# Where the products of the next block's input stand on VectorE, and one step less for two projection units, in a chunked-attention stage

## The chip, the cores and the metric

The kernel runs on one core of a Trainium2 chip. The metric is the time of one execution on the device in microseconds (us); lower is better. Of several runs of one kernel the median is taken. One execution is also recorded by the hardware profiler, and all durations of single instructions come from such a record. The engines are TensorE (PE in the profile; its weight loads are PEld), VectorE (DVE), ScalarE (ACT), GpSimd (POOL) and SyncE (SP), which here only issues DMAs.

## The reference

One layer over 2048 frames of width 1024. A normalised input feeds one projection; its first 512 columns go through a state-space layer, the other 1536 are queries, keys and values of chunked attention. Both outputs are normalised, go through one output projection, and a gated feed-forward network follows. What matters here is the input of the attention and the attention:

```python
h = rmsnorm(x, norm_mix_g[l])
proj = h @ w_in[l]
...
scores = jnp.einsum('bnqhd,bnkhd->bhnqk', qc, kb) / math.sqrt(HEAD_DIM)
scores = scores + bias[None, :, None, :, :]
scores = jnp.where(valid[None, None, :, None, :], scores, -1e30)
probs = jax.nn.softmax(scores, axis=-1)
out = jnp.einsum('bhnqk,bnkhd->bnqhd', probs, vb)
```

There are 8 heads of 64 columns; a frame attends to its own chunk of 64 frames and the 8 chunks before it. All of it is float32.

## The kernel before, in words

**Phases.** The kernel computes the state-space input first, then attention together with the state-space scan, then the output projection, the feed-forward network and the final norm. Every float32 matmul operand is split into a part `hi` (cast to a 32-bit format that PE takes in one pass) and the rest `lo`; `mm3` (L145 to L148) makes three matmuls of each product: hi by hi, hi by lo, lo by hi. All PE instructions of this stage are kept in program order; for the other engines a scheduler decides the order of their queues when the kernel is built, by when it thinks that each operand is ready. An instruction can so be queued long before the place at which the program names it.

**Attention in steps.** `att_phase` (L687) works through 128 steps: 4 blocks of 512 frames, 4 pairs of heads in each, 2 heads of a pair, 4 groups of 128 queries. Block *b* has the steps 32*b* to 32*b*+31; "step 23 of block 1" is step 55. Step *s* does, in this order (`ORDER`, L52):

- the scores of step *s* (L848): two to four matmuls into the PSUM tile `sc`, of which there is one; then on DVE one instruction (L874) that adds the bias and takes the minimum `mn` of each row; then on ACT the exponential (L877). Scores are negated, so that the minimum is what is subtracted.
- after the fourth query group of a head, the product with the values (L895), three steps late, and the scaling of a finished pair (L919), four steps late.
- the transposes of step *s*-2 (L880): up to five on PE into the one tile `pt`, then a cast `pth` on ACT (L892) and a difference `ptl` on DVE (L893).
- pieces of the units that are due (L984 to L986).

**Units.** A `Unit` (L665) is a generator with a number of pieces, a first step and a step by which it is over; `advance` (L672) runs as many pieces in each step as the share of its steps that has gone by. They fill PE between scores and transposes:

- `qk_unit(sb, pr)` (L754): queries and keys of one pair of heads, 2 x 8 pieces of three matmuls. When the key half is over, ACT casts the keys into `k2` (L799) and DVE forms the difference (L800); the scores of that pair read `k2`. In block 0 a scaling (L784) goes before it.
- `v_unit(sb, fh)` (L807): values of four heads, 16 pieces of six matmuls.
- `hT_unit(sb, q0, q1)` (L724): the normalised input of block `sb`, eight tiles `q` of 128 rows. It loads a tile (into `xt`, or two at a time into `raw`), and multiplies it on DVE by the gain and the row scale, in place (L749: the product); ACT casts it to `hi` (L750) and DVE forms `lo` (L751). Its first three tiles are due in steps 20 to 22 of the block before, the other five in steps 24 and 25. The next block's first `qk_unit` begins in step 24 and reads tiles 0 to 2 there, 3 to 5 in step 25, 6 and 7 in step 26.
- `ssm_front` (L561) and `ssm_back` (L636): eight parts of the scan. Each has a few matmuls (`pj<-U,Bst`, `pj<-U,Tm`), copies on ACT, and about 37 us of small operations on POOL (L598 to L610), of which the last eight (L609, L610 on 434 columns) are the long ones.

The tuple `CUT` (L50) says at which steps of a block the units begin and end: pair 0 from -8 to -2, values' first half to 2, pair 1 to 7, pair 2 to 13, values' second half to 19, pair 3 (the last) to 24. `CUTL` is the same for the last block but ends pair 3 at 23. Pair 3's scores begin at step 24.

## Time and profile before

| | us |
|---|---|
| median of 3 runs | 2253.35 |
| lowest and highest | 2246.03, 2255.34 |
| the profiled execution | 2247.43 |
| its span (first to last instruction) | 2245.7 |
| attention stage, 128 steps, from about | 136 to 702 |

A row of the timeline is: start in us from the span's start, duration in us, engine, line, operation, what it writes and reads, shape, count, and in brackets how long the engine was idle before it and what ended that. A row of a group has a count, and minimum, median and maximum duration in ns. A row of the windows has the length of the window, then the busy time and number of instructions of PE, PEld, DVE, ACT and POOL, then the clock of PE that was granted (1.00 is full), the share of the DMA engines and GB/s. Matmuls overlap, so that the distance from one start to the next says more than the duration of one: 128x512 matmuls last 0.39 us and start 0.23 us apart.

### The profile page before, as it was taken

The numbers are of one execution on the slowest core, as the hardware profiler recorded it, in microseconds if no ns is written. First come the engines' busy times: TensorE is split into PE (matmuls) and PEld (weight loads), VectorE is DVE, ScalarE is ACT, GpSimd is POOL, SyncE is SP. The second block draws the span as 40 slices with busy tenths as digits, with TensorE's granted clock in tenths as the row PEclk, the third lists the DMA queues.
The fourth block names the chain that finished last, engine by engine and source line by source line (L and its number), as shares of the span: only waits on it lengthen the run. The fifth ranks groups of instructions, "written<-read, shape, count | busy, mean of one in ns | idle before, by whom it ended". The sixth has DMA issues, their size and how long they took to land.

```text
span 2245.7 us, 30154 instructions
## 1 busy us (share of the span) xinstructions
PE 2155.6 (96%) x10632; PEld 1817.4 (81%) x10632; DVE 1543.3 (69%) x2706; ACT 1004.6 (45%) x1667; POOL 352.4 (16%) x827
## 2 busy tenths in 40 slices
PE   8998899999997999999999999999999999999997
PEld 6777788899986788788888887888888788888886
DVE  7756666555557766777766678767666477689776
ACT  5455555556557642443333335333333343353322
POOL 2246576656500000000000000000000100000000
PEclk9999999999998999999999999999999999999999
DMA  8878876666652435845655557646333395465652
GB/s 281 251 244 275 280 220 204 202 192 199 190 166 99 155 113 181 288 136 155 198 168 194 191 182 268 210 144 213 117 100 112 122 383 192 160 228 177 220 175 76
DMA packets 194744, 430.16 MB, mean 192 GB/s; under 512 B 19872, under 2 KB 38352, under 8 KB 187488
## 3 DMA queue, kind: packets, MB, share of 16 engines
q1 hardware_dynamic: 186944, 403.32, 54.4%
q0 software_dynamic: 7648, 24.92, 3.6%
q8 instruction: 83, 1.36, 0.2%
q14 instruction: 69, 0.57, 0.1%
HBM read 288.95 MB, written 131.10 MB: 187 GB/s over the span
## 4 chain that ended last, share of the span: by engine, by line
PE 81%; DVE 7%; DMA 4%; ACT 3%; issue 2%; SPq 0%; DVEq 0%; ACTq 0%
PE X L76 20%; PE ps L76 19%; PE Y L76 10%; PE pf L76 10%; PE big L76 7%; PE W L76 5%; PE pj L76 4%; PE pt L79 2%; PE sc L76 2%; DMA lo<-hc 1%; DMA xt<-in_xt 1%; DVE ptl L893 1%; DMA x<-xt 0%; DVE s L874 0%; DVE lo L153 0%
## 5 line engine op out<-in xcount | busy, mean ns | idle before, releaser
L76 PE MATMUL X<-hi,c 128*128 128x512 f32 x1408 | 449.8, 390 | 6.7 <-DVE c L153 3.9
L76 PE MATMUL ps<-hd,hd 128*128 128x512 f32 (+1 forms) x1968 | 428.1, 379 | 3.1 <-DVE hd L153 2.0
L76 PEld LDWEIGHTS ps<-hd,hd 128*128 128x128 f32 x1968 | 356.4, 188 | 73.3 <-DVE hd L153 2.7
L76 PEld LDWEIGHTS X<-hi,c 128*128 128x128 f32 x1408 | 264.5, 188 | 63.2 <-DVE c L153 4.7
L76 PE MATMUL X<-lo,c 128*128 128x512 f32 x704 | 274.4, 390 | 0.0
L153 ACT CAST hd<-hd 128x1536 fp32r<-128x1536 f32 (+1 forms) x106 | 147.5, 1394 | 229.9 <-DMA hd<-hq 175.5
L76 PE MATMUL Y<-hi,c 128*128 128x512 f32 x704 | 224.8, 390 | 3.1 <-DVE u L1421 2.5
L153 DVE TENSOR_TENSOR hd<-hd 128x1536 fp32r<-128x1536 f32 (+1 forms) x106 | 174.0, 1643 | 38.0 <-ACT hd L153 37.7
L153 DVE TENSOR_TENSOR c<-S,c 128x512 fp32r<-128x512 f32 x176 | 120.8, 687 | 100.1 <-ACT c L153 99.8
L1525 POOL DMA_DIRECT2D hd<-hq x7 | 5.3, 755 | 1161.5 <-PE X L76 1148.8
L1417 ACT COPY u<-X 128x512 f32<-128x512 f32 x132 | 77.3, 586 | 197.7 <-PE X L76 197.7
L153 ACT CAST c<-S 128x512 fp32r<-128x512 f32 x176 | 109.4, 621 | 120.5 <-PE Y L76 61.6
L76 PE MATMUL big<-m,woh 128*128 128x512 f32 x512 | 160.1, 394 | 0.0
L76 PEld LDWEIGHTS Y<-hi,c 128*128 128x128 f32 x704 | 132.4, 188 | 31.9 <-DVE u L1421 3.3
L1559 DVE TENSOR_TENSOR acc<-acc,ps 128x512 f32<-128x512 f32 x196 | 129.6, 680 | 37.3 <-PE ps L76 37.1
L76 PEld LDWEIGHTS X<-lo,c 128*128 128x128 f32 x704 | 132.4, 188 | 27.4
L76 PE MATMUL pf<-hi,w 128*128 128x512 f32 x416 | 149.3, 411 | 0.0
L153 ACT CAST c<-raw 128x512 fp32r<-128x512 f32 x132 | 82.2, 623 | 147.7 <-PE Y L76 70.6
L76 PE MATMUL Y<-lo,c 128*128 128x512 f32 x352 | 137.2, 390 | 0.0
L893 DVE TENSOR_TENSOR ptl<-pt,pth 128x640 fp32r<-128x640 f32 (+3 forms) x152 | 98.2, 646 | 55.2 <-ACT pth L892 53.8
L877 ACT ACTIVATE s<-s,mn 128x640 f32<-128x640 f32 (+4 forms) x128 | 98.0, 765 | 61.1 <-DVE mn L874 57.7
L892 ACT CAST pth<-pt 128x640 fp32r<-128x640 f32 (+3 forms) x152 | 83.6, 550 | 84.2 <-PE pt L79 79.5
(448 smaller groups left out, 4267.9 us busy)
## 6 DMA issues: line engine op xcount, KB each, us to landing
w<-wss SPq DMA_DIRECT2D x36, 1024.0 KB, 6.1
hq<-g SPq DMA_DIRECT2D x140, 256.0 KB, 2.1
hd<-hq SPq DMA_DIRECT2D x35, 768.0 KB, 4.4
hd<-wc SPq DMA_DIRECT2D x35, 768.0 KB, 5.9
raw<-in_w_gate SPq DMA_DIRECT2D x44, 512.0 KB, 3.7
raw<-in_w_up SPq DMA_DIRECT2D x44, 512.0 KB, 4.1
wc<-px SPq DMA_DIRECT2D x66, 256.0 KB, 3.4
wss<-w SPq DMA_DIRECT2D x12, 1024.0 KB, 6.0
```

The costliest lines, as they stand in the source:

```text
L76: return self.tc.keep_in_program_order(self.tc.nc.tensor.matmul(*a, **b))
L79: return self.tc.keep_in_program_order(self.tc.nc.tensor.transpose(*a, **b))
L153: return nc.scalar.copy(hi, raw), nc.vector.tensor_tensor(lo, raw, f32(hi), op=ALU.subtract)
L877: nc.scalar.activation(s[:, :nk], s[:, :nk], AF.Exp, bias=mn[:], scale=-1.0, accum_out=sums[sb, pr][:, hh, qp : qp + 1])
L892: nc.scalar.copy(pth[:, a:b, qp, :], pt[:, a:b, :])
L893: nc.vector.tensor_tensor(ptl[:, a:b, qp, :], pt[:, a:b, :], f32(pth[:, a:b, qp, :]), op=ALU.subtract)
L1417: nc.scalar.copy(u[:], ps[:])
L1525: (nc.gpsimd if aside else nc.sync).dma_start(f32(lo), src.rearrange("g p c -> p g c"))
L1559: V.tensor_tensor(a, a, ps[:], op=ALU.add)
```

## The change

Three things change, all in the attention stage. L749, the product of the next block's input, is put behind the latest L874 that the program has named at that point, in DVE's queue: the minimum of the step in which `hT_unit` is advanced. The values' second half ends at step 18 in place of 19, and pair 3 runs from step 18 to 23 in place of 19 to 24. And the last block takes the same cuts as the others, so that its pair 3 has the steps 18 to 23 in place of 19 to 23. No computation is added or left out.

```diff
-CUT = -8, -2, 2, 7, 13, 19, 24
-CUTL = -8, -2, 2, 7, 13, 19, 23
+CUT = -8, -2, 2, 7, 13, 18, 23
...
-                nc.vector.scalar_tensor_tensor(xt, xt, k.gm[:, q : q + 1], S["rsn"][:, ts], op0=ALU.mult, op1=ALU.mult)
+                with tc.issue_after(k.least):
+                    nc.vector.scalar_tensor_tensor(xt, xt, k.gm[:, q : q + 1], S["rsn"][:, ts], op0=ALU.mult, op1=ALU.mult)
...
-            nc.vector.tensor_tensor_reduce(
+            ins = nc.vector.tensor_tensor_reduce(
                 s[:, :nk].rearrange("p (a b) -> p a b", a=nch), ps[:, :nch, :half],
                 hd.nb[:, nk - 1 :: -1].rearrange("p (a b) -> p a b", a=nch), 1.0, 3e38, ALU.add, ALU.min, mn[:])
+            k.least = ins.ins
...
-            C = CUT if sb < NSB - 1 else CUTL
+            C = CUT
```

`issue_after` asks the scheduler to place the instructions of its block later in the queue of the same engine than the one it names. It adds an order, and no semaphore.

## Prediction
> **What bounds the kernel now.** I read the page first: one engine fills the span.

> ```profile
> span 2245.7 us, 30154 instructions
> PE 2155.6 (96%) x10632; PEld 1817.4 (81%) x10632; DVE 1543.3 (69%) x2706; ACT 1004.6 (45%) x1667; POOL 352.4 (16%) x827
> ```

> TensorE (PE) is busy 96% of the span, so a scheduling edit can only win back moments in which PE stands still or runs slowly. The change acts in the attention stage alone. I cut that stage into its four blocks; the cuts are the starts of the instructions number 32, 64 and 96 of L874, which runs once a step. The busy times stand in the order PE, PEld, DVE, ACT, POOL.

> ```profile
> 267.00:421.00 154.00, 144.80 (x881) 130.35 (x880) 100.27 (x165) 86.50 (x176) 101.41 (x233) 0.98 0.70 216
> 421.00:558.00 137.00, 136.69 (x867) 124.81 (x866) 78.21 (x141) 78.86 (x158) 87.70 (x235) 1.00 0.67 202
> ```

> Block 1 (first row) and block 2 do the same attention work; block 2 leaves PE 0.3 us idle, block 1 leaves 9.2 us (154.00 less 144.80) and has a lower granted clock (0.98). So block 1 is where something is to be had. Next, the view of L749, the product that the change moves.

> ```profile
> L749 DVE SCALAR_TENSOR_TENSOR xt<-xt,g_mix,rsn x12: 741/751/1549, 214.9 to 390.2; 128x512 f32<-128x512 f32 x12
> L749 DVE SCALAR_TENSOR_TENSOR raw<-raw,g_mix,rsn x12: 740/745/2132, 237.4 to 392.7; 128x512 f32<-128x512 f32 x12
> ```

> The last products start at 392.7 us, in block 1, though what they make is block 3's input and block 3 starts at 558 us. The products run wherever their input lands and DVE's queue has them, not where the step order puts them. The timeline shows what that does in step 2 of block 1:

> ```profile
> 279.30 2.13 DVE L749 SCALAR_TENSOR_TENSOR raw<-raw,g_mix,rsn 128x512 f32<-128x512 f32 x1
> 281.42 1.07 POOL L609 TENSOR_TENSOR fx<-X,a 128x434 f32<-128x434 f32 x1
> 282.17 0.87 DVE L749 SCALAR_TENSOR_TENSOR raw<-raw,g_mix,rsn 128x512 f32<-128x512 f32 x1
> 282.96 0.81 DVE L893 TENSOR_TENSOR ptl<-pt,pth 128x640 fp32r<-128x640 f32 x1
> 283.83 1.26 PE L79 MATMUL pt<-ident,s 128*128 128x128 f32 x5 [3.11 <-DVE ptl L893]
> ```

> PE waits 3.11 us for `ptl`, which stands in DVE's queue behind two products (2.13 and 0.87 us) that nobody needs for another 90 us. Then the last pair's projection. In blocks 0 and 1 it ends in step 23, and step 24's scores read its keys at once; the rows are block 0, then block 1:

> ```profile
> 227.86 0.58 SPq L654 DMA_DIRECT2D y<-U  x1
> 232.01 0.69 DVE L784 TENSOR_TENSOR yt<-pf,rsn 128x512 f32<-128x512 f32 x1 [0.28 <-PE pf L76]
> 232.95 0.34 SPq L566 DMA_DIRECT2D U<-u  x1
> 233.38 1.40 DVE L800 TENSOR_TENSOR k<-yt,k 64x512 fp32r<-64x512 f32 x2 [0.68 <-ACT k L799]
> 234.17 0.30 PE L76 MATMUL sc<-k,q2h 128*128 128x128 f32 x1 [2.20 <-issue]
> 239.59 3.64 PE L76 MATMUL pj<-U,Bst 128*128 128x256 f32 x8 [2.61 <-DMA Bst<-bsts]
> ...
> 375.00 1.08 DVE L749 SCALAR_TENSOR_TENSOR xt<-xt,g_mix,rsn 128x512 f32<-128x512 f32 x1
> 376.00 2.98 DVE L751 TENSOR_TENSOR lo<-raw,hi 128x512 fp32r<-128x512 f32 x2
> 379.02 0.68 DVE L800 TENSOR_TENSOR k<-pf,k 64x512 fp32r<-64x512 f32 x1
> 379.76 0.63 PE L76 MATMUL sc<-k,q2h 128*128 128x320 f32 x1 [4.09 <-DVE k L800]
> ```

> In block 0 PE waits 2.20 us while the keys are evacuated (L784, L799, L800); in block 1 it waits 4.09 us, because L800 stands behind one product and two `lo` differences. The two long waits of block 1 cost more than themselves. The column before the last two is the granted clock:

> ```profile
> 284.00:287.30 3.30, 3.30 (x11) 2.81 (x11) 3.23 (x6) 1.51 (x3) 1.23 (x2) 0.50 0.51 118
> 379.60:382.90 3.30, 3.14 (x11) 2.81 (x12) 2.74 (x6) 1.72 (x3) 3.20 (x4) 0.50 0.53 196
> ```

> After each of them some 3.3 us run at half clock, which is 1.7 us of lost work.

> **The change part by part.** No instruction is added or removed but the order; the queue behind each L749 and the steps of two units move.

> *Early products go (L749 behind this step's L874).* Block 2's eight products leave steps 1 to 4 of block 1. The 3.11 us wait and its half clock go: **-4.8 us**. Block 2 at the same steps has next to no PE idle, so nothing else is late there. Ends: 0 (if `ptl` is late for another reason) and -4.8; I take -4.8, since the two products in front of `ptl` last 3.0 us of the 3.11.

> *Last pair a step sooner (18 to 23).* The key evacuation of 1.4 us and what is before it then lies beside step 23. Block 1: 4.09 and 1.7 go, **-5.8 us**. Block 0: the 2.20 goes, but 2.8 us later PE stands before `U,Bst` anyway, for a transfer: `U<-u` is issued only when the store `y<-U` has landed (issued 227.86, next 232.95). PE comes to it sooner and waits longer, unless the store moves too. It was issued behind the queries' copies of the last pair on SP's queue, which now come a step sooner, but the matmuls that fill `U` (step 20) have three projection groups more ahead of them. Ends 0 and -2.2; I take **-1.0**, the middle, as no row is nearer to one end.

> *Values' second half in five steps in place of six.* PE does the same matmuls; denser steps 13 to 17 have PE as their limit: 0. It also starts the scan of steps 16 to 25 a little later on POOL (79% of the half lies before its matmuls in step 16, against 68%), which counts below. For block 3 the pair takes five steps in place of four with the same end: 0. Of the DMAs, the weight loads of the moved units and the copies of keys and queries go one step earlier on SP's queue; the landing that PE waits for in these steps is the one of block 0 above.

> *What is late next: step 23 without a projection.* Scores and transposes alone then. Block 3 has such steps today; the three rows below it are block 2's scan matmuls:

> ```profile
> 661.59 0.41 PE L76 MATMUL sc<-k,q2h 128*128 128x320 f32 x1 [1.12 <-DVE mn L874]
> ...
> 520.37 1.89 PE L76 MATMUL pj<-rsn,Bst 128*128 128x256 f32 x8
> 525.63 0.59 PE L76 MATMUL pj<-U,Tm 128*128 128x256 f32 x2
> 528.90 0.50 PE L76 MATMUL sc<-k,q2h 128*128 128x320 f32 x1
> ```

> The next scores wait 1.12 us for the minimum that reads the one `sc` tile. Block 2 has 1.89 us of scan matmuls in step 23 as cover (and 3.3 us, from 525.63 to 528.90, in step 24), block 0 narrow scores. So **+1.1** in block 1; ends 0 and 2.2 over the blocks.

> *What the products cost where they now stand.* It is an order in DVE's queue, no new semaphore. Behind a product that is late stand, on DVE, its difference `lo`, then `ptl` and the next minimum; on ACT, its cast `hi` and the exponentials behind it; PE waits for all of these. Each block's products 3 to 5 wait for the minimum of step 24, 6 and 7 for that of step 25, and step 25's matmuls need `lo` 3 to 5. In block 1 (PE rows of its step 24, then prices on DVE, then the scan on POOL):

> ```profile
> 384.85 0.71 PE L79 MATMUL pt<-ident,s 128*128 128x128 f32 x5
> 385.31 0.48 PE L76 MATMUL pf<-hi,w 128*128 128x512 f32 x1
> 387.48 0.37 PE L76 MATMUL sc<-k,q2h 128*128 128x320 f32 x1
> 388.13 0.40 PE L76 MATMUL pj<-pth,v 128*128 128x512 f32 x1
> ...
> 380.69 0.82 DVE L874 CUSTOM_DVE_ANT_0 s<-sc,nba 128x640 f32<-128x640 f32 x1 [0.26 <-PE sc L76]
> 387.33 0.69 DVE L751 TENSOR_TENSOR lo2x<-xt,hi2x 128x512 fp32r<-128x512 f32 x1
> 387.94 0.82 DVE L893 TENSOR_TENSOR ptl<-pt,pth 128x640 fp32r<-128x640 f32 x1
> 388.67 0.74 DVE L749 SCALAR_TENSOR_TENSOR raw<-raw,g_mix,rsn 128x512 f32<-128x512 f32 x1
> 383.23 1.95 DVE L751 TENSOR_TENSOR lo1x<-xt,hi1x 128x512 fp32r<-128x512 f32 x1
> 385.10 1.54 DVE L749 SCALAR_TENSOR_TENSOR xt<-xt,g_mix,rsn 128x512 f32<-128x512 f32 x1
> 374.48 1.06 POOL L609 TENSOR_TENSOR fx<-X,a 128x434 f32<-128x434 f32 x1
> 384.70 1.39 POOL L610 TENSOR_TENSOR X<-X,fx 128x434 f32<-128x434 f32 x1
> ...
> L598 POOL TENSOR_TENSOR st<-X,a 128x128 f32<-128x128 f32 x56 | 28.1, 502 | 162.3 <-ACT X L584 158.6
> ```

> PE from the end of step 24's scores to `lo` 5: five transposes 0.46, nine matmuls 2.17, four scores 0.65, transposes 0.46, seven matmuls at 0.24: 5.4 us. DVE in that stretch: two minima at 0.9, one `ptl` 0.82, three products and three differences. With POOL silent that is 2.6 + 3 x 0.74 + 3 x 0.69 = 6.9 us, 1.5 more than PE gives. But the last eight large scan operations run from 374.48 to 386.1, and beside them a product or difference lasts about 1.5 us (1.95, 1.54, and 2.98 for two). Without its wait, PE reaches step 24 some 4 us sooner, so the whole stretch lies beside them: 2.6 + 6 x 1.5 = 11.6 us, that is **+6.2 us** of waiting. Ends: 1.5, and 2.6 + 6 x 2.13 - 5.4 = 10.0 by the longest row, with 1.7 of half clock if it is one wait. I take 6.2: the rows from this very stretch are the nearest. Block 0 keeps its cost, for its products already follow that minimum and POOL is idle there. Block 2 gets eight products that it did not have, with 1.89 and 3.3 us of scan matmuls as cover and a scan that is then at its small operations (last row, 0.50 us each): **+0.7**, ends 0 and 5.

> The sum: -4.8 - 5.8 - 1.0 + 1.1 + 6.2 + 0.7 = **-3.6 us** on the profiled execution's 2247.43 us (its span 2245.7 and 1.7 around it), so 2243.8. The three runs shown have their median at 2253.35, 5.9 above that execution; carried over, 2249.7.

> [...]

> **The rivals.** *All waits go, nothing comes.* Then -4.8 - 5.8 - 2.2 = -12.8, and 2240.6. For it: DVE is busy only 65% of block 1 (100.27 of 154), and products 0 to 2 now fall into steps 20 to 22, before the crowd. Against it: the 11.6 us worked out above.

> *Slower: the products starve beside the scan.* All ten operations of products 3 to 7 last 2.13 us in blocks 1 and 2. Six of them make 10.0 us of waiting in block 1 and, against 8.7 us of PE work in block 2 (5.4, and 3.3 of scan matmuls), 6.7 there; four more are 4 x 1.4 = 5.6 in each block; half clock 1.7 in each. With 1.1 for step 23 that is 32, less 12.8: +19, and 2272. It decides where the ten operations average 1.3 us in both blocks (then the cost passes 12.8), and 1.7 us is needed for 0.5%. Against it: block 2's scan operations are the small ones, and block 1's last four have 16 matmuls of the next step as cover.

> *The order on DVE is not what holds PE.* Other work takes the place of the early products in front of `ptl`, and block 0 waits for its transfer: only block 1's step 23 changes, for the crowd of step 24. Then about -1, 2252.

> **How the numbers follow.** Chances: forecast 0.50, all gain 0.22, slower 0.14, nothing 0.14. About 0.5% (11.3 us) is what a measurement of this kernel can tell from no change. Faster by more: the full gain and a tail of the forecast, 0.24. Slower by more: the third case and a little, 0.15. Within: 0.61. The range reaches from the full gain with some of the runs' spread, 2237, to 2262, which takes in the upper ends of the two unknown costs (3.8 more in block 1, 4.3 in block 2) and leaves the third case out.

> **What would show it.** Right: no L749 between 250 and 345 us; no PE wait near step 2 of block 1; L800 of the last pair before step 24's scores; in step 25 of block 1 waits of PE on `lo` (L751), some 6 us together, with L749 and L751 near 1.5 us. Wrong: those waits absent (then the gain is whole), a wait of over 10 us there or in block 2, or the wait for `ptl` in block 1 with no product in front of it. A longer wait for `Bst` in block 0 shows how much of the 2.2 was given back.

## The result, and the profile after

| | before | after |
|---|---|---|
| median of 22 runs each, us | 2250.2 | 2256.27 |
| lowest and highest, us | 2246.03, 2258.62 | 2251.1, 2262.07 |
| profiled execution, us | 2247.43 | 2251.1 |
| its granted clock of PE | 0.988 | 0.986 |

The ratio of the times is 1.0019, with a 95% interval of 1.0010 to 1.0028: the changed kernel is slower, by 2 to 6 us, which is inside the 0.5% that the prediction called no change. The forecast was 3.6 us faster. On the profiled pair the difference is 3.6 us of span (2249.3 less 2245.7). Both profiled executions lie under their medians, by 2.8 us before and 5.2 us after; the one after is the fastest of its 22. In the changed kernel's rows, what was L52 to L748 before has a number one lower, and what was L877 or later one higher.

The head of the page after:

```profile
span 2249.3 us, 30152 instructions
PE 2159.1 (96%) x10632; PEld 1820.0 (81%) x10632; DVE 1541.7 (69%) x2706; ACT 1005.1 (45%) x1667; POOL 354.7 (16%) x827
```

Blocks 1 and 2 of the changed kernel, cut at the starts of instructions number 32, 64 and 96 of L874 (windows view; length, then PE, PEld, DVE, ACT, POOL, clock):

```profile
270.37:422.34 151.97, 144.51 (x880) 129.90 (x879) 88.43 (x155) 85.22 (x172) 99.30 (x224) 0.98 0.68 208
422.34:561.47 139.13, 137.23 (x867) 124.55 (x866) 85.96 (x153) 80.49 (x160) 87.62 (x231) 1.00 0.64 202
```

The prediction's rows of before were cut at rounded times, up to 0.8 us early; from the same instructions block 1 of the kernel before lasts 153.73 us and block 2 136.94. So block 1 is 1.8 us shorter than before, block 2 is 2.2 longer, and block 1 begins 2.6 later (270.37, the start of step 32's minimum, for 267.82). Two losses stand around one gain. The products do go where the change sends them (groups of L749 in the changed kernel):

```profile
L749 DVE SCALAR_TENSOR_TENSOR xt<-xt,g_mix,rsn x12: 744/751/1106, 217.3 to 526.5; 128x512 f32<-128x512 f32 x12
L749 DVE SCALAR_TENSOR_TENSOR raw<-raw,g_mix,rsn x12: 734/746/1545, 236.7 to 535.6; 128x512 f32<-128x512 f32 x12
```

The last one starts at 535.6 us, in block 2, in place of 392.7.

**Block 0.** The timeline of the changed kernel around step 24 of block 0 (rows picked from it):

```profile
223.64 0.38 SPq L653 DMA_DIRECT2D y<-U  x1
...
230.67 0.44 PE L78 MATMUL pt<-ident,s 128*128 128x128 f32 x2 [0.74 <-DVE ptl L894]
...
232.05 1.40 DVE L800 TENSOR_TENSOR k<-yt,k 64x512 fp32r<-64x512 f32 x2
...
232.76 1.04 SPq L802 DMA_DIRECT2D ks<-k  x2
...
232.83 0.45 PE L75 MATMUL sc<-k,q2h 128*128 128x128 f32 x1 [1.73 <-issue]
...
233.86 0.44 SPq L730 DMA_DIRECT2D raw<-in_xt  x1
...
234.02 0.87 PE L78 MATMUL pt<-ident,s 128*128 128x128 f32 x3 [0.53 <-DVE ptl L894]
...
234.39 0.46 SPq L565 DMA_DIRECT2D U<-u  x1
...
241.11 1.10 PE L75 MATMUL pj<-U,Bst 128*128 128x256 f32 x4 [2.38 <-DMA Bst<-bsts]
...
264.33 0.50 PE L75 MATMUL pf<-w,hi 128*128 128x256 f32 x2 [0.95 <-DMA w<-wss]
```

The wait of 2.20 us for the keys has not gone. Three waits stand in its place, 0.74, 1.73 and 0.53, together 3.0. The longest is still the wait for the keys: the profile shows no releaser for it ("issue"), but it ends at 232.83, just after the first of the two L800 (232.05, some 0.7 us each), as it did before (233.38, then 234.17). Step 23 without a projection is too thin to cover the evacuation, and the prediction had priced that for block 1 alone. The store `y<-U` is issued 4.2 us sooner than before (223.64 for 227.86). Yet `U<-u`, which needs it, is issued 1.4 us later (234.39 for 232.95): the key store and a load of the input stand ahead of it in SP's queue now, and the key store waits for the keys. PE stands before `U,Bst` nearly as long as before (2.38 for 2.61), but starts it 1.5 us later (241.11 for 239.59): that is most of what block 0 loses. In the other 1.0 us lies a new wait of 0.95 us for a weight load (last row).

**Start of block 1.** No PE wait is left near step 2. But look at step 4, first in the changed kernel and then in the kernel before:

```profile
290.55 2.65 ACT L583 COPY X<-pj 64x256 f32<-64x256 f32 x7 [5.77 <-DMA XG<-X]
292.10 0.70 PE L75 MATMUL pj<-U,Tm 128*128 128x256 f32 x2 [1.09 <-ACT X L583]
```

```profile
289.91 3.03 ACT L584 COPY X<-pj 64x256 f32<-64x256 f32 x8 [0.23 <-PE pj L76]
293.75 0.59 PE L76 MATMUL pj<-U,Tm 128*128 128x256 f32 x2
```

Before, the copies into `X` waited for PE. Now PE waits for the copies, and these for `XG<-X`, the transfer that ends the scan begun at `U,Bst`. From the start of `U,Bst` to the issue of the last `XG` the scan takes 2.1 us less than before (43.2 for 45.3), but that transfer takes 2.2 us more (6.1 for 4.0), so it lands 1.6 us later (290.45 for 288.81). Why it takes longer is not shown; the DMA engines' share meanwhile was 0.90, against 0.71 before. The 3.11 us won at the start of the block meet a date that PE does not set.

**End of block 1.** The timeline of the changed kernel, steps 23 to 25 (rows picked):

```profile
375.56 0.42 PE L75 MATMUL sc<-k,q2h 128*128 128x320 f32 x1 [1.51 <-DVE mn L874]
...
376.27 0.69 DVE L800 TENSOR_TENSOR k<-pf,k 64x512 fp32r<-64x512 f32 x1
377.00 0.82 DVE L874 CUSTOM_DVE_ANT_0 s<-sc,nba 128x640 f32<-128x640 f32 x1
...
378.37 1.40 POOL L608 TENSOR_TENSOR fx<-X,a 128x434 f32<-128x434 f32 x1
...
380.24 1.52 DVE L751 TENSOR_TENSOR lo<-xt,hi 128x512 fp32r<-128x512 f32 x1
381.69 1.54 DVE L749 SCALAR_TENSOR_TENSOR raw<-raw,g_mix,rsn 128x512 f32<-128x512 f32 x1
381.82 0.50 PE L75 MATMUL pf<-lo,w 128*128 128x512 f32 x1 [1.18 <-DVE lo L751]
383.16 1.74 DVE L751 TENSOR_TENSOR lo<-raw,hi 128x512 fp32r<-128x512 f32 x1
384.95 0.50 PE L75 MATMUL pf<-lo,w 128*128 128x512 f32 x1 [2.17 <-DVE lo L751]
386.57 0.79 PE L75 MATMUL pf<-lo,w 128*128 128x512 f32 x1 [0.63 <-DVE lo L751]
```

The 4.09 us wait for the keys is gone and L800 is early. In its place stand 1.51 for the minimum, and 1.18 + 2.17 + 0.63 = 3.98 for `lo`, with three products and differences of 1.5 to 1.7 us beside the scan's long operations on POOL.

**Block 2** (timeline of the changed kernel, step 22):

```profile
520.01 0.75 DVE L749 SCALAR_TENSOR_TENSOR xt<-xt,g_mix,rsn 128x512 f32<-128x512 f32 x1 [3.24 <-DMA xt<-in_xt]
...
521.28 0.80 DVE L894 TENSOR_TENSOR ptl<-pt,pth 128x640 fp32r<-128x640 f32 x1
...
522.14 0.77 PE L78 MATMUL pt<-ident,s 128*128 128x128 f32 x5 [1.19 <-DVE ptl L894]
```

The third product holds DVE's queue for 3.24 us until its transfer has landed; `ptl` and PE wait behind it. By the kernel, `xt` has two buffers, so this load waits for the first tile to be used up, and held products use it up later: the differences of the first two tiles start at 512.12 and 512.72, the load is issued at 514.67 and lands 5.2 us later.

**The sum, term by term.** Measured values are differences, after less before, of the distances between the starts of L874 of the two profiled executions:

| stretch | predicted, us | measured, us |
|---|---|---|
| to the end of block 0 | -1.0 | +2.55 |
| block 1, steps 0 to 5 | -4.8 | -5.42 + 1.36 = -4.06 |
| block 1, steps 6 to 31 | -5.8 + 1.1 + 6.2 = +1.5 | +2.29 |
| block 2 | +0.7 | +2.19 |
| rest | 0 | +0.66 |
| sum | -3.6 | +3.63 |

(-5.42 is steps 0 to 3, +1.36 the two steps with `U,Tm`.) The rest, which the change hardly touches, came out up to 10 us longer than before in the records of the kernels below; so the rows of one pair of records are no proof, and the experiments matter. Against the forecast, block 0 is off by 3.6 us, half of all; block 2 by 1.5, the other three rows by 0.7 or 0.8 each.

### The profile page after: what moved, and what is told of

Same layout as the page of the kernel before. It is cut to its first block, busy times and chain, and to the rows that moved or that the text cites. A ratio compares the mean times of both kernels' runs of the same rounds, so it can differ in the third digit from the quotient of the medians.

```text
span 2249.3 us, 30152 instructions
## 1 busy us (share of the span) xinstructions
PE 2159.1 (96%) x10632; PEld 1820.0 (81%) x10632; DVE 1541.7 (69%) x2706; ACT 1005.1 (45%) x1667; POOL 354.7 (16%) x827
## 3 DMA queue, kind: packets, MB, share of 16 engines
q8 instruction: 83, 1.36, 0.2%
## 4 chain that ended last, share of the span: by engine, by line
PE 75%; DVE 6%; issue 5%; DMA 4%; POOL 4%; ACT 2%; SPq 0%; DVEq 0%; ACTq 0%; POOLq 0%
PE X L75 20%; PE ps L75 17%; PE Y L75 10%; PE pf L75 8%; PE big L75 6%; PE W L75 5%; PE pj L75 4%; PE sc L75 2%; PE pt L78 2%; DMA lo<-hc 1%; DMA hd<-wc 1%; POOL st L597 1%; POOL X L600 1%; DVE lo L152 1%; POOL X L599 1%
## 5 line engine op out<-in xcount | busy, mean ns | idle before, releaser
L893 ACT CAST pth<-pt 128x640 fp32r<-128x640 f32 (+3 forms) x152 | 83.8, 551 | 78.6 <-PE pt L78 74.4
```

What stands on the lines that cost most here:

```text
L893: nc.scalar.copy(pth[:, a:b, qp, :], pt[:, a:b, :])
```

## The experiments

The theory: order and cuts win what was predicted at the waits themselves, and lose it again at the thin step 23 and at three other places: the scan's transfers (`U,Bst`, `U,Tm`), the products beside the long scan operations, and the third product's load. The first rival: the new cuts cost it all, and holding the products is a plain gain of about 4 us. Letters A to D in the expectations mean the theories of that run alone.

### The two halves of the change

Order alone: the old `CUT` and `CUTL` are put back in the changed kernel.

> The products queued behind their minimum, with the old cuts. Theory A (the change loses in three places: block 0's steps 22 to 24, products beside the scan in steps 24 and 25 of block 1, the third product's load in block 2): the start of block 1 gains about 4 us; the waits for the last pair's keys stay, about 2 us in each of blocks 0 and 1; step 25 of block 1 still waits on lo for some 4 us, step 22 of block 2 about 1 us; in all within 2 us of the kernel before (ratio 0.999 to 1.001). Rival B (the earlier cuts cost it all, the held products are pure gain): 4 us or more faster than before, ratio 0.998 or less.

Measured: 2251.57, ratio 1.0006 (0.9995 to 1.0018). Near the end of block 1 PE waits 1.32 us for the keys in place of 4.09, but then 3.57 for `lo`. Its timeline at `U,Tm`:

```profile
290.38 3.02 ACT L584 COPY X<-pj 64x256 f32<-64x256 f32 x8 [7.08 <-DMA XG<-X]
291.93 0.70 PE L76 MATMUL pj<-U,Tm 128*128 128x256 f32 x2 [2.40 <-ACT X L584]
```

Cuts alone: the new `CUT` for all blocks in the kernel before, products free.

> The new cuts, with the products free as before. Theory A: the wait of 3.1 us at the start of block 1 stays; block 0 loses 2 to 3 us as in the changed kernel (scan input issued behind the key stores, more half clock); in block 1 the wait of 4.1 us for the keys goes and some 1.5 us come in step 23; in all 0 to 2 us slower than before (ratio 1.000 to 1.001). Rival B: the cuts carry the whole loss and what the held products gain comes on top, so about 8 us slower, ratio 1.0035.

Measured: 2254.19, 1.0012 (1.0000 to 1.0024). The 3.11 us wait is gone here too, though the products are free, and against the expectation: the scheduler's order came out otherwise. `U,Bst` waits 4.77, `U,Tm` 2.51.

Neither half is a gain; by their ratios 0.06% and 0.12% make about the 0.19% of the whole, though each interval reaches down to no loss. The first rival falls: held products alone do not gain 4 us. In both, the time won at the start of block 1 ends in front of `U,Tm`.

### The third product's load

```diff
-HTA = -12, -9
+HTA = -13, -9
```

(The first three products are due a step earlier.)

> The changed kernel, but the first three products of a block due one step earlier, so that the third one's load has a step more to land. Theory A: DVE's idle time before the third product (3.24 us in block 2, 1.27 in block 1) falls under 1 us and PE's wait of 1.19 us for ptl in step 22 of block 2 goes; 1 to 2 us faster than the changed kernel (ratio to before 1.001). If that load is not what holds ptl: no difference, ratio 1.002.

Measured: 2253.98, 1.0011 (0.9999 to 1.0023). The wait of 1.19 us in block 2 is gone, and block 2 is 0.7 us longer than before in place of 2.19. The waits for `lo` in block 1 stay (1.18 and 2.17). So this cost is real and about 1.5 us in the records; the time alone (1.0011 for 1.0019, with intervals that overlap) does not show it.

### The products beside the scan

First, the scan's last operations taken away: `ssm_front` leaves out the last carry of its fourth part (`b == 3`), whose state-space result is therefore incomplete.

> The changed kernel, with the last carry of the fourth scan part left out (the eight long operations on POOL that lie beside step 24 of block 1), so that part of the state-space output is not the reference's. Theory A: L749 and L751 in steps 24 and 25 of block 1 last about 0.75 us in place of 1.1 to 1.7; PE's waits on lo there (1.18 + 2.17 + 0.63 us) fall to 1 us or less in all and the half clock after them goes; 4 to 6 us faster than the changed kernel (ratio to before about 0.9995). Rival (DVE has too much to do there whatever POOL does): waits of 2.5 us or more stay and the time falls by less than 2 us.

Measured: 2251.79, 1.0006 (0.9995 to 1.0016). Timeline at step 25 of block 1 (L753 and L755 are here the product and the difference):

```profile
384.31 0.69 DVE L755 TENSOR_TENSOR lo<-xt,hi 128x512 fp32r<-128x512 f32 x1
...
388.21 0.50 PE L75 MATMUL pf<-lo,w 128*128 128x512 f32 x1 [0.23 <-DVE lo L755]
```

Then the same without leaving anything out, by beginning that scan part two steps sooner:

```diff
-SX = 4, 24, 35, 48, 61, 74, 87, 100
+SX = 4, 24, 35, 46, 61, 74, 87, 100
```

> The changed kernel with one edit: the front of the fourth scan part starts at step 46 in place of 48, so that its long operations on POOL should be over before products 3 to 7 of block 1 run. Theory A (the products are slow there because of the scan beside them): L749 and L751 around 380 us fall from about 1.5 us to 0.75, the waits on lo in step 25 (1.18, 2.17 and 0.63 us) fall below 1 us together, and the kernel gains 3 us: ratio 1.0005. Theory B (it is the order behind the minimum that makes lo late): the waits stay at 3 us or more together and the ratio is 1.0019.

Measured: 2252.79, 1.0006 (0.9995 to 1.0017). Its only wait for `lo` in that stretch, and the group of the differences that lasted 956 ns in the median in the changed kernel (706 here):

```profile
386.83 0.50 PE L75 MATMUL pf<-lo,w 128*128 128x512 f32 x1 [0.22 <-DVE lo L751]
```

```profile
L751 DVE TENSOR_TENSOR lo<-raw,hi x12: 684/706/1087, 238.0 to 535.4; 128x512 fp32r<-128x512 f32 x12
```

Steps 22 to 31 of block 1 are 4.5 us shorter than in the changed kernel. Two different edits take the waits away together with the slow operations, so the waits come from the scan beside them and not from the order behind the minimum. By the ratios this price is some 3 us (1.0019 less 1.0006, times 2250), though the intervals overlap; and it is not inherent to the change.

### The scan's date

Parts 1 and 2 of the scan a step later, in the changed kernel and in the kernel before (`SX` 25 for 24 and 36 for 35, `SY` 37 for 36):

> The changed kernel, with the front of the second scan part one step later (step 25), the front of the third one step later (36) and the back of the second one step later (37). Theory C: the 4 us that the held products win at the start of block 1 are given back, because PE next stands before the scan chain (load of U, U,Bst in step 24 of block 0, 39 us on POOL, XG, U,Tm in step 4 of block 1), which takes 51 to 54 us whatever PE does. Then the waits at U,Bst (2.4 us) and U,Tm (1.1 us) fall under 0.5 us each, and the kernel is 2.5 to 5 us faster than the changed one (ratio to before 0.9985 to 1.001). Rival D (the early gain is kept, and the loss lies in the later blocks alone): ratio stays at 1.002.

> The kernel before, with the same three scan units one step later. Theory C: its wait at U,Bst (2.61 us) and the half clock after it go, the wait of 3.11 us behind the early products stays; 1 to 3 us faster than before (ratio 0.999). Rival D: no difference (1.000).

Measured: 1.0006 (0.9992 to 1.0019) with the change, 1.0026 (1.0014 to 1.0038) without it. In the changed kernel the wait at `U,Bst` shrinks to 0.43, and the one at `U,Tm` grows to 3.44: it moves along. The kernel before loses its wait at `U,Bst` too and is all the same slower than unmoved, with 2.70 us in front of `pt` where it was 3.11 and 4.09 for the keys as ever. An expectation of a gain without the change falls.

Only the end later (`SX` 36 for 35, `SY` 37 for 36, `U,Bst` left in step 24):

> The changed kernel with the matmuls behind the first long scan (U,Tm) and the front of the next part one step later (37 for 36, 36 for 35), its beginning (U,Bst) left at step 24. Theory A (what the held products win at the start of block 1 is taken back because the scan from U,Bst to U,Tm lasts 51 to 54 us whatever PE does): the wait in front of U,Tm, 1.09 us in the changed kernel, goes to 0 to 0.3, the wait in front of U,Bst stays at 2 to 5, and the kernel gains 1 to 2 us: ratio to the kernel before 1.0010 to 1.0015. Theory B (that wait is copies queued on ScalarE for another reason): the wait stays at about 1 us one step later and the time is that of the changed kernel, 1.0019.

Measured: 2254.22, 1.0015 (1.0004 to 1.0026). The wait at `U,Tm` is gone and one of 4.15 stands at `U,Bst`, as theory A has it; the time does not tell the theories apart.

All moves together (`HTA` -13, `SX` 25, 36 and 46, `SY` 37), and the same with the old cuts:

> The changed kernel with what the runs so far point to: the three scan units later, the first products one step earlier, and the front of the fourth scan part two steps earlier (46), so that its long operations are over before step 24 of block 1. Theory A with C: waits on lo in step 25 of block 1 at 1 us or less, no wait for ptl in block 2, none at U,Bst and U,Tm; 6 to 9 us faster than the changed kernel (ratio to before 0.998 to 0.9995). If the waits only move on to other transfers: 1.001 or more.

> The same as the run before it, with the old cuts. Theory A with C: the waits for the last pair's keys (some 2 us each in blocks 0 and 1) stay, the waits of step 23 go, so within 2 us of the run before it. Rival B (the cuts cost the change its time): 3 us or more faster than the run before it.

Measured: 2247.37, **0.9985 (0.9974 to 0.9996)** with the whole change, the best of all kernels and better than the one before; 2250.84, 0.9991 (0.9978 to 1.0005) with the old cuts. In the first the waits for `lo` fell under 0.4 us each and the one for `ptl` in block 2 went, but the wait at `U,Tm` stayed with 2.28, which was not expected. The old cuts came out 3.5 us slower by the medians, which neither of their theories has; rival B, that the cuts cost the change its time, falls, but the intervals overlap. The moves of the first were never put into the kernel before; so what the change itself adds to them is not shown. Then the same as the first, but with `U,Bst` back in step 24:

> The kernel with all moves (first products a step earlier, fourth scan part from step 46, second part's front at 36 and U,Tm at 37), but with the second part of the scan begun at step 24 as in the changed kernel, not at 25. Theory A (U,Bst to U,Tm lasts 51 to 54 us whatever PE does): the wait in front of U,Bst comes back (2 to 5 us for 0.46) and the one in front of U,Tm falls from 2.28 to below 0.5; together about as much waiting as with all moves or 1 us more: ratio 0.9985 to 0.9993. Theory B (the two waits have nothing to do with each other): the wait in front of U,Tm stays at 2.3 and the one in front of U,Bst is added: ratio 0.9995 to 1.0005.

Measured: 2248.93, 0.9991 (0.9978 to 1.0005). Timeline:

```profile
239.93 3.75 PE L75 MATMUL pj<-U,Bst 128*128 128x256 f32 x8 [5.01 <-DMA Bst<-bsts]
...
294.14 0.59 PE L75 MATMUL pj<-U,Tm 128*128 128x256 f32 x2
```

The wait at `U,Tm` (2.28 with all moves) is gone, and 5.01 stand at `U,Bst`: theory A. From `U,Bst` to `U,Tm` it was 51.0 to 54.2 us in the kernel before, in the changed one, and in the six others of these that keep that scan's steps (e1 to e4, e10, e11). In the kernel before PE was the later one there; to the landing of the last `XG` it was 49.2 to 52.4 us in these eight.

### Block 0

Old cuts in block 0 alone:

```diff
-            C = CUT
+            C = CUT if sb else CUT0
```

> The changed kernel with the old cuts (values' second half to 19, last pair 19 to 24) in block 0 alone. Theory A (in block 0 a thin step 23 and the load U<-u issued later behind the key stores make the change lose 2 to 3 us there): U<-u is issued within 0.5 us of the landing of y<-U again, U,Bst starts 1 to 2 us earlier than in the changed kernel, and the ratio is 1.0007 to 1.0013. Theory B (block 0 only loses by where a half clock stretch falls): U,Bst starts at the same time as in the changed kernel, and the ratio is 1.0019.

Measured: 2256.08, 1.0016 (1.0004 to 1.0029). `U<-u` is issued as soon as `y<-U` has landed, as theory A says, and `U,Bst` starts at 240.13, 1.0 us sooner; but the time shows no gain, with an interval that holds the numbers of both theories, and `U,Tm` waits 3.50 for `XG`. So SP's queue delays that load (by 1.65 us in the changed kernel, from the landing of `y<-U` at 232.74 to 234.39). Taking this away did not bring the time back here, since `U,Tm` starts 2.1 us later than in the changed kernel all the same.

### An earlier beginning, with and without the change

`SX` 23 for 24 and `SY` 18 for 20, so that the first scan is begun earlier:

> The changed kernel with the first scan begun earlier: the matmuls that end the scan part before it (and so the store y<-U) at step 18 in place of 20, U,Bst at step 23 in place of 24; everything else as in the changed kernel. Theory A (the early gain of block 1 is taken back because the scan from U,Bst to U,Tm lasts 51 to 54 us whatever PE does, and U,Bst waits only for y<-U and U<-u): y<-U is issued some 7 us earlier, the waits in front of U,Bst (2.38 us) and U,Tm (1.09) both fall below 0.5, and the kernel gains about 3 us: ratio 1.0003 to 1.0008. Theory B (the waits there are a matter of what else PE has; something else is late next): the waits move but do not get shorter together, ratio 1.0015 to 1.0022.

Measured: 2251.79, 0.9999 (0.9988 to 1.0010). Timeline:

```profile
219.84 0.36 SPq L653 DMA_DIRECT2D y<-U  x1
...
227.87 0.39 SPq L565 DMA_DIRECT2D U<-u  x1
...
235.27 3.47 PE L75 MATMUL pj<-U,Bst 128*128 128x256 f32 x8 [3.40 <-DMA Bst<-bsts]
...
291.80 0.59 PE L75 MATMUL pj<-U,Tm 128*128 128x256 f32 x2
```

The time falls as theory A says, by even more, and the wait at `U,Tm` is gone. Its other half missed: the wait at `U,Bst` grew to 3.40. `y<-U` landed at 222.96, but `U<-u` was issued 4.9 us later, since four copies of queries and a load of the input stand ahead of it on SP.

With the other two moves added (`HTA` -13, `SX` 46), with and without the change:

> The changed kernel with the first scan begun earlier (18 and 23 as above), the first products of a block a step earlier and the fourth scan part from step 46. Theory A (the costs found so far add up: 3 us of scan beside products, 1 to 2 us of the third product's load, 3 us at U,Bst and U,Tm): no wait over 1.2 us between 235 and 400 us but the minimum of step 23, and 0.9970 to 0.9980. Theory B (they do not add up: what is won at one place is lost at the next wait): 0.9985 to 0.9995, no better than the kernel with all moves so far.

> The kernel before (old cuts, products not held) with the same three moves. Theory A (with the scan out of the way the change is worth its two waits, 3.11 and 4.09 us, and some half clock): they stay here, and this kernel stands at 0.9990 to 1.0000, 3 to 5 us behind the changed kernel with the same moves. Theory B (the change is worth nothing or less even then): the two are within 1 us of each other, or this one is ahead.

Measured: 2249.9, 0.9996 (0.9987 to 1.0005) with the change, 2257.12, 1.0024 (1.0013 to 1.0034) without it. The costs do not add up to the 0.9970 to 0.9980 that theory A gave the first; here theory B's "no better than so far" holds, with 5.64 us in front of `U,Bst`. The kernel without the change was expected at 0.9990 to 1.0000 and is slower than that. Between the two kernels, which differ by the change alone, lie 7 us, more than expected, and their intervals are apart. The kernel without the change, at steps 6 and 7 of block 1 and at step 24:

```profile
305.45 0.89 DVE L749 SCALAR_TENSOR_TENSOR xt<-xt,g_mix,rsn 128x512 f32<-128x512 f32 x1 [5.60 <-DMA xt<-in_xt]
306.87 0.80 DVE L893 TENSOR_TENSOR ptl<-pt,pth 128x640 fp32r<-128x640 f32 x1
307.72 1.33 PE L79 MATMUL pt<-ident,s 128*128 128x128 f32 x5 [3.70 <-DVE ptl L893]
...
383.03 0.69 DVE L800 TENSOR_TENSOR k<-pf,k 64x512 fp32r<-64x512 f32 x1
383.77 0.42 PE L76 MATMUL sc<-k,q2h 128*128 128x320 f32 x1 [3.50 <-DVE k L800]
```

A product that nobody needs for another 70 us waits 5.60 us for its transfer with `ptl` behind it, and the keys are late as before. These are the two waits that the change is meant for. With the scan's steps as they were it costs 0.19%; with these moves it gains. Some of the 7 us may be the moves' own doing: the wait of 5.60 us is not in the kernel before.

## Why the prediction was wrong, point by point

The step that failed first is the price of block 0: the prediction let the 2.20 us go and took -1.0, and the runs show +2.55. The second is "nothing else is late there", behind the -4.8. The signs that the prediction had listed for being right nearly all came, so they did not test the sum.

- **-4.8, early products go.** The mechanism was right: no product runs between 250 and 345 us, PE waits for nothing where the 3.11 us were, steps 0 to 3 are 5.42 us shorter. (Between the two products stood a third instruction, L917 with 0.68 us, which the prediction's excerpt leaves out.) The step that failed is "nothing else is late there". It was read off block 2, whose scan is timed otherwise; in block 1 the landing of `XG` is late 5 us further on. The start of `U,Tm` is the test, for all that comes before it is in it: against the kernel before it was 1.65 us sooner in the changed kernel, and between 1.8 sooner and 2.4 later in e1 to e4, e10 and e11. The prediction had it 5.8 sooner. In the pair of records the row itself misses by only 0.7 us (-4.06), in the records of those six by 2.2 to 4.9.
- **-1.0 in block 0.** Wrong in sign (+2.55, and between +1.1 and +4.9 in those six). "The 2.20 goes" failed: 1.73 of waiting for the keys is left, and "block 0 narrow scores" was no cover, so that the thin step has 3.0 us of waiting in all. And the store did move, 4.2 us, which was the condition for the better end, but SP's queue held the load behind it, and `U,Bst` started 1.5 us later. The prediction named that the copies of keys go earlier on SP's queue and did not ask what is then behind them. What part of the +2.55 the cuts have stays open, since e11 lost 2.2 there with the old ones (and also waited for a weight load, 0.82 us).
- **-5.8, +1.1 and +6.2 at the end of block 1.** Right in mechanism and nearly in size: wait for the keys gone, 1.51 for the minimum, net +2.29 for +1.5. The +6.2 was mis-sized: 3.98 was waited for `lo`. Of the six operations that it priced at 1.5 us each, three took 1.5 to 1.7 and three 0.8 to 1.1, 1.28 in the mean. e4 and e10 show the cause.
- **+0.7 in block 2.** Mis-sized, +2.19. The sum had priced products 3 to 7 and not the load of the third, 1.19 us of PE's wait and about 1.5 us in all by e3.
- **The rivals.** "All waits go" is out, as the waits for `lo` came. "The products starve" named the right cause with the wrong price: at most 1.74 us, not 2.13 for each, and in block 1 alone. "The order on DVE is not what holds PE" had the transfer of block 0 right, and its 2252 is nearest of all to the time; but that is luck, as its reason, other work in front of `ptl`, is not what was seen.

These misses and 0.7 us in the rest make the 7.2 us between -3.6 and +3.6. The waits were read well one by one. What the sum lacked was the question, asked of each gain, which later date that PE does not set it runs into.

Left open: why the kernel before gets slower by moving its first scans later (e6). Its record is 1.7 us shorter up to the start of block 2 and longer only behind block 2, where nothing was changed.

## What to carry to other kernels

A wait taken from the busiest engine is worth only what is left of it at the next meeting with a chain that does not run on that engine; find that meeting (here a scan of some 50 us with transfers at both ends) before the gain is booked. When work is held back to a later place, price what already runs beside that place and which buffer it gives back later. And when a change loses, look whether what it collides with can move: the same change cost 0.19% with the scan's steps as they were and, with scan and products out of each other's way, belongs to the only one of the fifteen kernels tried that beats the one before by more than its interval (which reaches up to 0.9996).

## What the runs showed of the hardware

```profile
228.79:232.20 3.41, 1.57 (x7) 0.77 (x6) 2.83 (x8) 2.19 (x7) 0.00 (x0) 0.99 1.00 359
232.20:235.60 3.40, 2.24 (x8) 1.92 (x9) 2.90 (x8) 3.11 (x9) 0.00 (x0) 0.50 0.90 286
235.60:239.00 3.40, 3.13 (x8) 1.93 (x6) 3.23 (x6) 1.62 (x4) 0.00 (x0) 0.50 0.91 276
```

In the first row PE was busy 1.57 of 3.41 us, with no single wait over 1.73, and 6.8 us at half clock followed. By the prediction's way of counting (1.7 us lost after a wait of 3 us) there would have been none.

**The same wait does not always cost the same.** Where these stretches start differs from record to record: counted from the span's start in steps of 3.41 us, it is 0.4 us past a step before and 3.2 us after. In block 0 of e7, waits of 1.73 and 0.77 us were followed within 1 us by 3.4 us of half clock (128x512 matmuls started 0.43 us apart in place of 0.23); in e2, e3 and e12, after waits of 1.73 and 0.78 us at the same place, none came before the next long wait at `U,Bst`. By the mean granted clock of a stretch (twice what it lacks to 1, times the length), the kernel before spent 10.2 us at half clock between 205 and 655 us and the changed one 17.1; the others lay between 3.4 and 20.5. From 655 us to the end, where the kernels do nearly the same work, it was 29.8 us before, the least of all, 34.0 after, and 34.3 to 51.6 in the others. At most half of such a number is lost time (less where PE would next have waited anyway), so records of nearly equal work can differ, by an estimate from these numbers, by up to 11 us by this alone (half of 51.6 less 29.8), and the record of before was a lucky one.

**An early issue into busy DMA engines gained little.** `y<-U` landed 5.1 us after its issue in the kernel before and 9.1 in the changed one (issued 4.2 sooner, landed 0.2 sooner); the share of the DMA engines was 1.0 in both meanwhile. In e13, issued at 219.84 with a share of 0.75, it landed after 3.1 us. That the load is the reason is argued and not shown.
